# First modulation of the last two pairs of k tiles: sums over partitions on VectorE with a 32x32 transpose, their first row on ScalarE

## The chip, the cores and the metric

The kernel runs on one core of one Trainium2 chip. The metric is the device time of one execution in microseconds (us). Five engines work side by side, each through a queue of its own that it takes in order: TensorE (PE, with its weight loads as PEld), VectorE (DVE), ScalarE (ACT), GpSimd (POOL) and SyncE (SP), which here issues nearly all transfers. An engine that comes to an instruction whose input is not there yet waits, and everything behind that instruction in its queue waits with it. A difference of 0.2% (1.9 us) is about what a measurement of this kernel can tell from no change.

## What is computed

One block of a decoder on 512 tokens of 1024 features, in float32. What matters here is its first step: a normalised input is scaled and shifted by vectors that come from a conditioning vector `c`, and the result `h` is projected.

```python
cs = jax.nn.silu(c)                                   # (1, 1024)
mod = cs @ ada_w[l] + ada_b[l]                        # (1, 6 * 1024)
sh_m, sc_m, gt_m, sh_f, sc_f, gt_f = jnp.split(mod, N_MOD, axis=-1)
h = modulate(rmsnorm(x, norm_mix_g[l]), sh_m, sc_m)   # h * (1 + scale) + shift
proj = h @ w_in[l]
...
h = modulate(rmsnorm(x, norm_ffn_g[l]), sh_f, sc_f)
```

`sh_m` and `sc_m` are needed before any projection can start; `sh_f` and `sc_f` only for the second half of the block. Everything after `proj` (retention, a short convolution, the merge, a feed-forward part) is untouched by the change.

## The kernel before

**Products in three parts.** Every float32 matrix is split into a rounded high part and the rest (names ending in `_h` and `_l`; for the activations `Hh` and `Hl`), and a product is made of three matmuls, low by high, high by low, high by high. TensorE works on these from the first microseconds to the last.

**The start, by pairs of k tiles.** The 1024 features of `h` are 8 k tiles of 128. Up to line 551 the kernel works on the first projections (two column tiles each of `c`, `u`, `b` and one of `k`, seven accumulators in all) by k tile, as the data come in: pair 0 (k tiles 0 and 1), then pairs 2, 4 and 6. In this part all five queues are in the order in which the program is written (`strict = True`, line 352, up to line 552): nothing is moved by a scheduler.

For a pair `j`, the columns of `ada_w` for its shifts and scales are 4 x 128 numbers wide, and each partition holds 8 of the 1024 rows. So the vector-matrix product is done in two steps:

- `ada_sum` (line 185): VectorE multiplies the first row by its factor in `cs` (`tensor_scalar_mul`, into a tile `acc_m`) and adds the other seven, one `scalar_tensor_tensor` each, 128x512. `some_sums` (line 478) spreads this over the loop: rows 0 and 1, then (behind the low part of k tile `j-2`) rows 2 and 3, then rows 4 to 7.
- `mod_sums` (line 396): TensorE sums over the partitions. `acc_m` is the stationary side, in four blocks of 128 columns, against a 128x128 tile of ones; the four results lie in the PSUM tile `mods`, by feature. In the trace each of these float32 matmuls has two records, so a pair has eight.

`mod_cols` (line 225) then makes the scale and shift of both k tiles from `mods` with three small VectorE instructions (`a_m`, `s_m`, `a_m`), ScalarE applies them (`h_hi` writes `Hh`, `h_full` the full `h` over the input tile `xT`), and VectorE takes the difference (`h_lo`, `Hl`).

The loop over `j` in (2, 4, 6) is short and its order is the order on every queue:

```python
        steps = products(j - 1)
        run(steps, 14)
        ...
        mod_sums(sums[j], both, j > 2)
        w_lo("c", j)
        mod_cols("m", j, mods.rearrange("p (i n) -> p i n", n=P)[:, :, 0])
        for k in (j, j + 1):
            h_hi(k)
            h_full(k)
        ...
        run(steps)
        some_sums(j + 2, 0, 2)
        h_lo(j)
        run(products(j))
```

`products(k)` are the 21 matmuls of k tile `k`, three parts of seven. In an even k tile the part with `Hl` comes last; in an odd one too, and the sums of the next pair over partitions stand on TensorE's queue just ahead of those last seven (`run(steps, 14)`).

**A second way to sum over partitions** exists further down for the second modulation and the gates: `quarters` (line 244) makes two small constant tiles (`quart_sum` 128x128 and `quart_own` 128x4), `quarter_sums` (line 254) sums 32 columns at a time behind a 32x32 transpose in one VectorE instruction (128x16 from 128x512), and one matmul with `quart_sum` and two small VectorE instructions finish it (`mod_whole`, line 265). `quarters` is called at line 837, in the later part.

Of the kernel before, what the change touches and what calls it, by code (L numbers as in the profile page):

```python
# [11 lines left out]
F32 = mybir.dt.float32  # L12
# [4 lines left out]
ALU = mybir.AluOpType  # L17
AX = mybir.AxisListType

P = 128  # L20
# [50 lines left out]
def block_kernel(ctx, tc, x, c, positions, ada_w, ada_b, norm_mix_g, w_in, conv_w, ret_w_out,  # L71
# [3 lines left out]
    pe, vec, act, pool, sync = (InTurn(tc, e) for e in (nc.tensor, nc.vector, nc.scalar, nc.gpsimd,  # L75
                                                        nc.sync))
    mm, transpose = pe.matmul, pe.transpose
# [5 lines left out]
    sp = ctx.enter_context(tc.tile_pool(name="sp", bufs=4))  # L83
# [15 lines left out]
    def aux(name, shape=None):  # L99
        return ps.tile(shape or [P, S], F32, tag="aux", bufs=2, name=name)  # L100
# [64 lines left out]
    cs = cp.tile([P, KT], F32, name="cs")  # L165
# [19 lines left out]
    def ada_sum(pieces, n, name, a=None, k0=0):  # L185

        first = a is None
        if first:
            a = sp.tile([P, n], F32, tag="adaacc", bufs=2, name=f"acc_{name}")
        for k, w in enumerate(pieces, k0):  # L190
            if first and k == k0:
                vec.tensor_scalar_mul(a, w, cs[:, k:k + 1])
            else:
                vec.scalar_tensor_tensor(a, w, cs[:, k:k + 1], a, ALU.mult, ALU.add)
        return a
# [7 lines left out]
    def ada_load(f, j):  # L203


        s0 = 0 if f == "m" else 3
        cols = slice(j * P, (j + 2) * P)
        ada_raw[f, j] = pieces = []
        for k in range(0, KT, 4):
            raw = wp.tile([P, 4, 2, 2 * P], F32, tag="raw", bufs=3, name=f"ada_{f}{j}_{k}")  # L210
            for q, i in ((q, i) for q in range(0, 4, 2) for i in range(2)):
                load_raw.last = sync.dma_start(raw[:, q:q + 2, i],
                                               aw6[:, k + q:k + q + 2, s0 + i, cols])
            pieces += [raw[:, q].rearrange("p s n -> p (s n)") for q in range(4)]

    def mod_scale(f, k, col):
        g = (R_GM if f == "m" else R_GF) + k
        vec.scalar_tensor_tensor(mod["a_" + f][:, k:k + 1], col, vecs[0][:, g:g + 1],
                                 mod["b_" + f][:, k:k + 1], ALU.mult, ALU.add)

    def mod_shift(f, k, cols, n):
        r = R_ADA + ADA["sh_" + f] // P + k
        vec.tensor_tensor(mod["s_" + f][:, k:k + n], cols, vecs[0][:, r:r + n], ALU.add)

    def mod_cols(f, j, pt):

        mod_scale(f, j, pt[:, 2:3])
        mod_shift(f, j, pt[:, 0:2], 2)
        mod_scale(f, j + 1, pt[:, 3:4])

    def mod_gains(f):

        r0 = R_ADA + ADA["sc_" + f] // P
        g0 = R_GM if f == "m" else R_GF
        vec.scalar_tensor_tensor(mod["b_" + f], vecs[0][:, r0:r0 + KT], 1.0, vecs[0][:, g0:g0 + KT],
                                 ALU.add, ALU.mult)
# [4 lines left out]
    QP = P // 4  # L241
    quart, own, mod_q = {}, {}, {}

    def quarters():
        quart["sum"] = cp.tile([P, 4, QP], F32, name="quart_sum")
        cols = sp.tile([P, QP], F32, tag="quart", bufs=1, name="quart_cols")
        vec.tensor_reduce(cols, ident.rearrange("p (q c) -> p c q", q=4), axis=AX.X, op=ALU.add)
        vec.tensor_copy(quart["sum"], cols.unsqueeze(1).to_broadcast([P, 4, QP]))
        quart["own"] = cp.tile([P, 4], F32, name="quart_own")
        vec.tensor_reduce(quart["own"], ident.rearrange("p (q c) -> p q c", q=4), axis=AX.X,  # L250
                          op=ALU.add)
        quart["f"] = cp.tile([P, 2 * D // QP], F32, name="quart_f")

    def quarter_sums(o, a):

        vec.tensor_reduce(o, a.rearrange("p (j c) -> p j c", c=QP), axis=AX.X, op=ALU.add,
                          apply_transpose=True)
# [86 lines left out]
    def w_load(k):  # L344
        for n in "cubk":
            cols = P if n == "k" else 2 * P
            w_raw[n, k] = scr(f"w_{n}0_{k}", F32, [P, 2, cols])
            load_raw.last = sync.dma_start(
                w_raw[n, k], wi[k * P:(k + 2) * P, COL[n]:COL[n] + cols].rearrange(
                    "(k p) n -> p k n", p=P))  # L350
# [31 lines left out]
    def x_by_feature(t, h, copy):  # L382
        for q in range(2):
            copy(xT[2 * h + q][:, :, t * P:(t + 1) * P], txs[t, h][:, 2 * q:2 * q + 2])

    kp, mods = aux("p_k00"), aux("mods")

    def mod_row(j, k, banks, first, cols=range(4)):


        for i in cols:
            mm(banks[i % 2][:, i * P:(i + 1) * P], lhsT=ada_raw["m", j][k][:, i * P:(i + 1) * P],
               rhs=cs[:, k:k + 1].to_broadcast([P, P]),
               start=first and (i == 0 or i == 1 and banks is apart), stop=False)

    def mod_sums(a, banks, first, cols=range(4)):

        for i in cols:
            mm(banks[i % 2][:, i * P:(i + 1) * P], lhsT=a[:, i * P:(i + 1) * P], rhs=ones32,
               start=first and i == 0, stop=i == 3 or i == 2 and banks is apart)  # L400

    apart, both = (mods, kp), (mods, mods)
# [23 lines left out]
    x_by_feature(2, 0, act.copy)  # L426
    x_by_feature(2, 1, act.copy)
    mod_gains("m")
    mod_row(0, 1, apart, False)
    a = ada_sum(ada_raw["m", 0][2:6], 4 * P, "m0", None, 2)  # L430
    x_by_feature(3, 0, act.copy)
# [18 lines left out]
    def w_hi(n, k):  # L450
        raws[n, k] = w_raw.pop((n, k))
        wt[n, k] = [slot(f"w_{n}0_{k}_{z}", F32R, raws[n, k].shape) for z in "hl"]
        act.copy(wt[n, k][0], raws[n, k])

    def w_lo(n, k):
        hi, lo = wt[n, k]
        vec.tensor_tensor(lo, raws.pop((n, k)), hi.bitcast(F32), ALU.subtract)
# [3 lines left out]
    def h_hi(k):  # L461

        h32[k] = xT[k // 2][:, k % 2]
        hist.append(act.activation(Hh[:, k, :], h32[k], AF.Identity,
                                   scale=mod["a_m"][:, k:k + 1], bias=mod["s_m"][:, k:k + 1]))
# [6 lines left out]
    def h_lo(k):  # L472
        hlast.append(vec.tensor_tensor(Hl[:, k, :], h32.pop(k), Hh[:, k, :].bitcast(F32),
                                       ALU.subtract))

    sums = {}

    def some_sums(j, k0, k1):

        if j < KT:  # L480
            sums[j] = ada_sum(ada_raw["m", j][k0:k1], 4 * P, f"m{j}", sums.get(j), k0)

    def products(k):
        ops = []
        parts = (0, 1, 2) if k % 2 else (1, 0, 2)
        for part in parts:
            x = (Hl if part == 2 else Hh)[:, k, :]
            for n, i in grp:
                w = wt[n, k - k % 2][1 if part == 0 else 0][:, k % 2, :]
                at = k == 0 and part == parts[0], k == KT - 1 and part == 2  # L490
                ops.append((gps[n, i], w[:, i * P:(i + 1) * P], x, at, (n, i)))
        if k == KT - 1:
            ops.sort(key=lambda o: grp.index(o[4]))
        if k == 0:
            order = {"c": 0, "u": 1, "b": 2, "k": 3}
            ops = sorted(ops[:14], key=lambda o: order[o[4][0]]) + ops[14:]
        for o, w, x, (first, last), _ in ops:
            yield mm(o, lhsT=w, rhs=x, start=first, stop=last)

    def run(steps, n=21):  # L500
        for _, _ in zip(range(n), steps):
            pass
# [27 lines left out]
    for j in range(2, KT, 2):  # L530
        if j + 2 < KT:
            ada_load("m", j + 2)
            w_load(j + 2)
        steps = products(j - 1)
        run(steps, 14)
        if j == 2:
            mod_row(j, 7, both, True)
        else:
            some_sums(j, 4, KT)
        for n in "cubk":  # L540
            w_hi(n, j)
        mod_sums(sums[j], both, j > 2)
        w_lo("c", j)
        mod_cols("m", j, mods.rearrange("p (i n) -> p i n", n=P)[:, :, 0])
        for k in (j, j + 1):
            h_hi(k)
            h_full(k)
        for n in "ubk":
            w_lo(n, j)
# [4 lines that stand above are left out]
        some_sums(j + 2, 2, 4)  # L554
        h_lo(j + 1)
# [278 lines left out]
    m_a = [None] * KT  # L834
    with tc.issue_after(hlast[-1].ins):
        mod_gains("f")
        quarters()
    merged = [None] * KT
    for p in range(KT // 2):
        sg = {}  # L840
# [46 lines left out]
    for p in range(KT // 2):  # L887
# [4 lines left out]
        for i, pt in proj(conv_w_out[0], 2 * p * P, conv_in, None, f"yb{p}"):  # L892
            f = 2 * p + i
# [300 lines left out]
    for h in range(2):  # L1194
# [15 lines left out]
        for t, cs in tm_gemm(ffn_w_down[0], af, f0, nf, h, groups, nf - 6, "dn", True):  # L1210
# [11 lines left out]
            i = 1 + cs.start // HS  # L1222
# [44 lines left out]
```

## Time and profile before

| | |
|---|---|
| time, median of 3 runs | 942.69 us (942.5 to 943.29) |
| time of the profiled execution | 942.61 us |
| its span in the profile | 940.8 us, so 1.81 us lie around the span |
| TensorE (PE) busy | 931.3 us, 99% of the span |
| TensorE weight loads (PEld) | 778.0 us, 83% |
| VectorE (DVE) busy | 634.2 us, 67% |
| ScalarE (ACT) busy | 359.9 us, 38% |
| granted TensorE clock, mean | 0.998 of full speed |
| VectorE busy from 20 to 40 us, from 40 to 60 us | 17.51 and 17.05 of 20 us |
| VectorE busy from 70 to 100 us | 29.8 of 30 us |

The profile is one execution. A line of the timeline gives the start of an instruction (or a group of like ones, xN), how long it took, its engine, the line of the kernel (L62 and L64 are the helper that records every operation), the operation, output<-input by tile names, and in square brackets how long the engine sat idle before it and what ended that. Matmuls overlap: a 128x512 matmul lasts 0.39 us in the records, and the next starts 0.23 us later, so the distance from start to start is the one to count. The same holds for VectorE and ScalarE, where the next independent instruction starts some 0.1 us before the end that is shown.

### The profile page before, as it was taken

The page shows a single profiled execution, that of the slowest core. Times are in us where ns is not written, and L with a number is a line of the kernel's source. Part 1 is how long each engine was busy: PE and PEld are TensorE (multiplying, and loading weights), DVE is VectorE, ACT ScalarE, POOL GpSimd, SP SyncE. Part 2 cuts the span into 40 slices and gives each one's busy share as a digit, 9 for nine tenths or more (in the row PEclk, how much of TensorE's full clock was granted, in tenths as well). Part 3 has the DMA queues.
Part 4 walks back from the last instruction along what each step waited for, and adds up shares of the span by engine and source line. Part 5 has one row for each costly group of instructions (what it writes and reads, how often), then busy time and mean ns, then how long its engine had stood idle before and what let it go on. Part 6 is the DMA issues. An engine that isn't in the chain of part 4 may idle for free.

```text
span 940.8 us, 11007 instructions
## 1 busy us (share of the span) xinstructions
PE 931.3 (99%) x4325; PEld 778.0 (83%) x4325; DVE 634.2 (67%) x977; ACT 359.9 (38%) x529; POOL 13.8 (1%) x34
## 2 busy tenths in 40 slices
PE   8999999999999999999999999999999999999997
PEld 8888888888888888888888888988888888888886
DVE  5889784898768756554674457668687546883346
ACT  7535432554444423222233236423443234433224
POOL 2000000000000000000000000000000000000000
PEclk9999999999999999999999999999999999999999
DMA  9943413321642346766463540446556652553202
GB/s 325 338 150 112 148 53 101 101 77 69 208 160 90 134 134 223 225 201 202 142 216 113 180 151 28 140 150 199 199 186 225 225 175 90 179 179 111 68 23 90
DMA packets 113491, 144.04 MB, mean 153 GB/s; under 512 B 4308, under 2 KB 93440, under 8 KB 112416
## 3 DMA queue, kind: packets, MB, share of 16 engines
q1 hardware_dynamic: 111472, 133.45, 43.3%
q0 software_dynamic: 1824, 9.63, 2.8%
q8 instruction: 34, 0.56, 0.2%
q10 hardware_dynamic: 144, 0.26, 0.1%
q14 instruction: 17, 0.14, 0.0%
HBM read 132.83 MB, written 10.49 MB: 152 GB/s over the span
## 4 chain that ended last, share of the span: by engine, by line
PE 97%; DMA 1%; DVE 1%; ACT 1%; issue 0%; SPq 0%; ACTq 0%
PE p_fu L64 13%; PE p_fg L64 12%; PE p_g L64 5%; PE p_yb L64 5%; PE p_v L64 5%; PE p_gb L64 5%; PE p_ya L64 5%; PE dn_t L64 5%; PE p_ga L64 5%; PE p_q L64 5%; PE p_k L64 4%; PE p_u L64 3%; PE p_b L64 3%; PE p_c L64 3%; PE dn_b L64 3%; PE dn L64 3%
## 5 line engine op out<-in xcount | busy, mean ns | idle before, releaser
L64 PE MATMUL p_fu<-Gh,w_fu_l 128*128 128x512 f32 x160 | 62.4, 390 | 0.0
L64 PE MATMUL p_fu<-Gl,w_fu_h 128*128 128x512 f32 x160 | 62.3, 389 | 0.0
L64 PE MATMUL p_fu<-Gh,w_fu_h 128*128 128x512 f32 x160 | 62.3, 389 | 0.0
L64 PE MATMUL p_fg<-Gh,w_fg_l 128*128 128x512 f32 x160 | 62.2, 389 | 0.0
L64 PE MATMUL p_fg<-Gh,w_fg_h 128*128 128x512 f32 x160 | 62.2, 389 | 0.0
L64 PE MATMUL p_fg<-Gl,w_fg_h 128*128 128x512 f32 x160 | 62.2, 389 | 0.0
L64 DVE TENSOR_TENSOR w_fg_l<-w_fg,w_fg_h 128x1024 fp32r<-128x1024 f32 x20 | 24.3, 1218 | 35.0 <-ACT w_fg_h L64 35.0
L64 ACT CAST w_fu_h<-w_fu 128x1024 fp32r<-128x1024 f32 x20 | 21.1, 1054 | 62.1 <-PE p_fu L64 39.6
L64 ACT ACTIVATE fg<-p_fg 128x512 f32<-128x512 f32 x22 | 13.1, 598 | 71.5 <-PE p_fg L64 71.5
L64 DVE TENSOR_TENSOR fg<-p_fu,fg 128x512 f32<-128x512 f32 x22 | 15.2, 690 | 35.5 <-PE p_fu L64 35.5
L64 DVE TENSOR_TENSOR w_b_l<-w_b,w_b_h 128x1024 fp32r<-128x1024 f32 x18 | 22.0, 1221 | 23.1 <-ACT w_b_h L64 23.1
L64 PEld LDWEIGHTS p_fu<-Gh,w_fu_l 128*128 128x128 f32 x160 | 30.0, 188 | 6.3
L64 PEld LDWEIGHTS p_fg<-Gh,w_fg_l 128*128 128x128 f32 x160 | 30.0, 188 | 6.3
L64 PEld LDWEIGHTS p_fg<-Gl,w_fg_h 128*128 128x128 f32 x160 | 30.0, 188 | 6.2
L64 PEld LDWEIGHTS p_fu<-Gh,w_fu_h 128*128 128x128 f32 x160 | 30.0, 188 | 6.2
L64 PEld LDWEIGHTS p_fg<-Gh,w_fg_h 128*128 128x128 f32 x160 | 30.0, 188 | 6.2
L64 PEld LDWEIGHTS p_fu<-Gl,w_fu_h 128*128 128x128 f32 x160 | 30.0, 188 | 6.2
L64 DVE TENSOR_TENSOR w_bl<-w_bl 128x512 f32<-128x512 f32 x32 | 22.0, 687 | 12.6 <-DMA w_bl<-in_ffn_w_down_dram 12.3
L64 DVE SCALAR_TENSOR_TENSOR acc_f<-ada_f,cs,acc_f 128x512 f32<-128x512 f32 x28 | 21.0, 750 | 8.8 <-DMA ada_f<-in_ada_w_dram 7.9
L64 ACT CAST sh<-sm 128x512 fp32r<-128x512 f32 (+3 forms) x32 | 14.7, 459 | 31.5 <-DVE sm L64 31.4
L64 DVE TENSOR_TENSOR w_fu_l<-w_fu,w_fu_h 128x1024 fp32r<-128x1024 f32 x20 | 24.4, 1220 | 3.4 <-ACT w_fu_h L64 3.4
L64 ACT CAST w_b_h<-w_b 128x1024 fp32r<-128x1024 f32 x18 | 18.9, 1049 | 19.1 <-issue 7.9
(429 smaller groups left out, 2716.5 us busy)
## 6 DMA issues: line engine op xcount, KB each, us to landing
w_fg<-in_ffn_w_gate_dram SPq DMA_DIRECT2D x11, 1024.0 KB, 5.3
w_fu<-in_ffn_w_up_dram SPq DMA_DIRECT2D x11, 1024.0 KB, 5.2
ada_m<-in_ada_w_dram SPq DMA_DIRECT2D x32, 256.0 KB, 5.3
w_bl<-in_ffn_w_down_dram SPq DMA_DIRECT2D x16, 512.0 KB, 4.7
blocks<-w_bl POOLq DMA_DIRECT2D x8, 1024.0 KB, 4.6
ada_f<-in_ada_w_dram SPq DMA_DIRECT2D x32, 256.0 KB, 4.6
w_t<-blocks SPq DMA_DIRECT2D x8, 1024.0 KB, 5.7
w_b<-in_ffn_w_down_dram SPq DMA_DIRECT2D x6, 1024.0 KB, 5.0
```

The lines of the kernel that those rows point to most:

```text
L64: self.last = op(*args, **kw)
```

## The change

It has three parts.

- The first row of `ada_sum` for pairs 4 and 6 is multiplied on ScalarE (`act.mul`) in place of VectorE (`tensor_scalar_mul`). The other rows stay.
- For pairs 4 and 6 the sum over partitions goes the second way: `quarter_sums` on VectorE, one matmul with `quart_sum` that has 16 columns, and two small VectorE instructions ahead of `mod_cols`. The four matmuls with ones go. Pair 2 stays as it was.
- `quarters` is called at the start, behind `mod_gains("m")`, no longer ahead of the second half.

```diff
@@ ada_sum
-            if first and k == k0:
+            if first and k == k0 and name in ("m4", "m6"):
+                act.mul(a, w, cs[:, k:k + 1])
+            elif first and k == k0:
                 vec.tensor_scalar_mul(a, w, cs[:, k:k + 1])
@@ the start
     mod_gains("m")
+    quarters()
     mod_row(0, 1, apart, False)
@@ new functions
+    def mod_quarters(j):
+        n = 4 * P // QP
+        part = sp.tile([P, n], F32, tag="mpart", bufs=1, name=f"mpart{j}")
+        quarter_sums(part, sums[j])
+        mm(mods[:, 0:n], lhsT=quart["sum"].rearrange("p q c -> p (q c)"), rhs=part, start=True,
+           stop=True)
+
+    def mod_own(j):
+        each = sp.tile([P, 4, 4], F32, tag="meach", bufs=1, name=f"meach{j}")
+        vec.tensor_tensor(each, mods[:, 0:16].rearrange("p (n q) -> p n q", q=4),
+                          quart["own"].unsqueeze(1).to_broadcast([P, 4, 4]), ALU.mult)
+        cols = sp.tile([P, 4], F32, tag="mown", bufs=1, name=f"mown{j}")
+        vec.tensor_reduce(cols, each, axis=AX.X, op=ALU.add)
+        mod_cols("m", j, cols)
@@ the loop over pairs
-        mod_sums(sums[j], both, j > 2)
-        w_lo("c", j)
-        mod_cols("m", j, mods.rearrange("p (i n) -> p i n", n=P)[:, :, 0])
+        if j == 2:
+            mod_sums(sums[j], both, False)
+            w_lo("c", j)
+            mod_cols("m", j, mods.rearrange("p (i n) -> p i n", n=P)[:, :, 0])
+        else:
+            mod_quarters(j)
+            w_lo("c", j)
+            mod_own(j)
@@ ahead of the second half
         mod_gains("f")
-        quarters()
```

Where this lands on the queues is seen at three places. The number behind a tile's name is that of its buffer. First ScalarE's queue in the round of pair 2, from the second k tile's `Hh` on (`xT_123` is the input of k tiles 2 and 3). Before:

```order
L62 ACTIVATE Hh<-xT_123,s_m,a_m 128x512
L62 ACTIVATE xT_123<-xT_123,s_m,a_m 128x512
L62 CAST w_c_4_h<-w_c_4_381 128x512
L62 CAST w_u_4_h<-w_u_4_383 128x512
L62 CAST w_b_4_h<-w_b_4_385 128x512
L62 CAST w_k_4_h<-w_k_4_387 128x256
```

The same place now:

```order
L62 ACTIVATE Hh<-xT_123,s_m,a_m 128x512
L62 ACTIVATE xT_123<-xT_123,s_m,a_m 128x512
L62 ACTIVATE acc_m_448<-ada_m_0_378,cs 128x512
L62 CAST w_c_4_h<-w_c_4_388 128x512
L62 CAST w_u_4_h<-w_u_4_390 128x512
L62 CAST w_b_4_h<-w_b_4_392 128x512
L62 CAST w_k_4_h<-w_k_4_394 128x256
```

The first row of pair 4 (`acc_m_448`) stands behind all four ACTIVATEs that apply the modulation of pair 2, and ahead of the high parts of pair 4's weights.

Second VectorE's queue at the same time, from the last weight of pair 2 to the shift of pair 4. Before:

```order
L62 TENSOR_TENSOR w_k_2_l<-w_k_2_335,w_k_2_h 128x256
L62 TENSOR_SCALAR acc_m_441<-ada_m_0_371,cs 128x512
L62 SCALAR_TENSOR_TENSOR acc_m_441<-ada_m_0_371,cs,acc_m_441 128x512
L62 TENSOR_TENSOR Hl<-xT_123,Hh 128x512
L62 SCALAR_TENSOR_TENSOR acc_m_441<-ada_m_0_371,cs,acc_m_441 128x512 x2
L62 TENSOR_TENSOR Hl<-xT_123,Hh 128x512
L62 SCALAR_TENSOR_TENSOR acc_m_441<-ada_m_4_376,cs,acc_m_441 128x512 x4
L62 TENSOR_TENSOR w_c_4_l<-w_c_4_381,w_c_4_h 128x512
L62 SCALAR_TENSOR_TENSOR a_m<-mods,vecs,b_m 128x1
L62 TENSOR_TENSOR s_m<-mods,vecs 128x2
```

The same place now:

```order
L62 TENSOR_TENSOR w_k_2_l<-w_k_2_342,w_k_2_h 128x256
L62 SCALAR_TENSOR_TENSOR acc_m_448<-ada_m_0_378,cs,acc_m_448 128x512
L62 TENSOR_TENSOR Hl<-xT_123,Hh 128x512
L62 SCALAR_TENSOR_TENSOR acc_m_448<-ada_m_0_378,cs,acc_m_448 128x512 x2
L62 TENSOR_TENSOR Hl<-xT_123,Hh 128x512
L62 SCALAR_TENSOR_TENSOR acc_m_448<-ada_m_4_383,cs,acc_m_448 128x512 x4
L62 TENSOR_REDUCE mpart_524<-acc_m_448 128x16
L62 TENSOR_TENSOR w_c_4_l<-w_c_4_388,w_c_4_h 128x512
L62 TENSOR_TENSOR meach_528<-mods,quart_own 128x16
L62 TENSOR_REDUCE mown_530<-meach_528 128x4
L62 SCALAR_TENSOR_TENSOR a_m<-mown_530,vecs,b_m 128x1
L62 TENSOR_TENSOR s_m<-mown_530,vecs 128x2
```

The first row is gone, and the second row, which reads what ScalarE writes, keeps its place ahead of `Hl`; three new instructions stand between the sums and the scale. The round of pair 4 looks the same with 4 and 6 in place of 2 and 4.

Third the start of VectorE's queue, where pair 0's sums begin. Before:

```order
L62 TENSOR_SCALAR x_136<-x_136,r_127 128x1024
L62 SCALAR_TENSOR_TENSOR b_m<-vecs 128x8
L62 TENSOR_SCALAR acc_m_264<-ada_m_0_138,cs 128x512
L62 SCALAR_TENSOR_TENSOR acc_m_264<-ada_m_0_138,cs,acc_m_264 128x512
L62 SCALAR_TENSOR_TENSOR acc_m_264<-ada_m_4_143,cs,acc_m_264 128x512 x2
```

The same place now:

```order
L62 TENSOR_SCALAR x_136<-x_136,r_127 128x1024
L62 SCALAR_TENSOR_TENSOR b_m<-vecs 128x8
L62 TENSOR_REDUCE quart_cols<-ident 128x32
L62 COPY quart_sum<-quart_cols 128x128
L62 TENSOR_REDUCE quart_own<-ident 128x4
L62 TENSOR_SCALAR acc_m_271<-ada_m_0_138,cs 128x512
L62 SCALAR_TENSOR_TENSOR acc_m_271<-ada_m_0_138,cs,acc_m_271 128x512
```

Three instructions of `quarters` now stand ahead of pair 0's first row.

## Rows read from the trace of the kernel before

**Rows 1.** The page: busy time of TensorE (us, share of the span, instructions), and the shares of the chain of work that ended last, by engine.

```profile
PE 931.3 (99%) x4325; PEld 778.0 (83%) x4325; DVE 634.2 (67%) x977; ACT 359.9 (38%) x529; POOL 13.8 (1%) x34
...
PE 97%; DMA 1%; DVE 1%; ACT 1%; issue 0%; SPq 0%; ACTq 0%
```

**Rows 2.** All waits of TensorE over the whole span: engine and what it was about to do <- who ended the wait: us in total, times, longest.

```profile
PE idle L64 <- POOL ident masks.py:199: 1.5, 1, 1.5
PE tx L62 <- DVE x L62: 0.9, 1, 0.9
PE p_c L62 <- ACT Hh L62: 0.4, 1, 0.4
PE y L64 <- ACT sh L64: 0.2, 1, 0.2
```

**Rows 3.** Timeline of TensorE in the rounds of pairs 2 and 4 (start us, us, engine, line, operation, output<-input, count).

```profile
33.79 0.62 PE L62 MATMUL p_c<-Hl,w_c_h 128*128 128x512 f32 x2
...
38.55 1.05 PE L62 MATMUL mods<-ones,acc_m 128*128 128x128 f32 x8
39.36 0.71 PE L62 MATMUL p_c<-Hl,w_c_h 128*128 128x512 f32 x2
39.91 0.63 PE L62 MATMUL p_u<-Hl,w_u_h 128*128 128x512 f32 x2
40.37 0.62 PE L62 MATMUL p_b<-Hl,w_b_h 128*128 128x512 f32 x2
...
44.24 0.62 PE L62 MATMUL p_c<-Hl,w_c_h 128*128 128x512 f32 x2
...
49.00 1.05 PE L62 MATMUL mods<-ones,acc_m 128*128 128x128 f32 x8
```

**Rows 4.** Timeline of VectorE in the same rounds.

```profile
31.05 0.48 DVE L62 TENSOR_SCALAR acc_m<-ada_m,cs 128x512 f32<-128x512 f32 x1
31.57 0.75 DVE L62 SCALAR_TENSOR_TENSOR acc_m<-ada_m,cs,acc_m 128x512 f32<-128x512 f32 x1
32.24 0.69 DVE L62 TENSOR_TENSOR Hl<-xT,Hh 128x512 fp32r<-128x512 f32 x1
...
34.89 3.11 DVE L62 SCALAR_TENSOR_TENSOR acc_m<-ada_m,cs,acc_m 128x512 f32<-128x512 f32 x4
37.91 0.68 DVE L62 TENSOR_TENSOR w_c_l<-w_c,w_c_h 128x512 fp32r<-128x512 f32 x1
...
39.78 0.15 DVE L62 TENSOR_TENSOR s_m<-mods,vecs 128x2 f32<-128x2 f32 x1
...
42.02 0.75 DVE L62 SCALAR_TENSOR_TENSOR acc_m<-ada_m,cs,acc_m 128x512 f32<-128x512 f32 x1
42.69 0.69 DVE L62 TENSOR_TENSOR Hl<-xT,Hh 128x512 fp32r<-128x512 f32 x1
...
45.35 3.11 DVE L62 SCALAR_TENSOR_TENSOR acc_m<-ada_m,cs,acc_m 128x512 f32<-128x512 f32 x4
```

**Rows 5.** Timeline of ScalarE in the same rounds.

```profile
31.91 0.82 ACT L62 ACTIVATE xT<-xT,s_m,a_m 128x512 f32<-128x512 f32 x1
...
39.96 0.82 ACT L62 ACTIVATE Hh<-xT,s_m,a_m 128x512 fp32r<-128x512 f32 x1 [4.23 <-DVE s_m L62]
...
42.37 0.81 ACT L62 ACTIVATE xT<-xT,s_m,a_m 128x512 f32<-128x512 f32 x1
43.09 0.61 ACT L62 CAST w_c_h<-w_c 128x512 fp32r<-128x512 f32 x1
```

**Rows 6.** Single tiles elsewhere in the span, with the kinds of instruction that the change adds: engine, operation, output<-input, count: duration in ns least/median/most, first and last start in us; shapes.

```profile
L64 ACT ACTIVATE o<-x,nf_r x4: 722/724/726, 926.3 to 936.4; 128x512 f32<-128x512 f32 x4
...
L64 DVE TRANSPOSE_TENSOR_REDUCE quart_f<-acc_f x4: 700/711/711, 362.8 to 429.9; 128x16 f32<-128x512 f32 x4
...
L64 DVE TENSOR_TENSOR mod_each<-mod_f,quart_own x1: 209/209/209, 450.7 to 450.7; 128x64 f32<-128x64 f32 x1
L64 DVE TENSOR_REDUCE mod_cols<-mod_each x1: 206/206/206, 451.2 to 451.2; 128x16 f32<-128x64 f32 x1
```

**Rows 7.** Timeline of TensorE where the second modulation's matmul with `quart_sum` (64 columns) stands between two projections.

```profile
449.16 0.33 PE L64 MATMUL mod_f<-quart_f,quart_sum 128*128 128x64 f32 x2
...
449.61 0.40 PE L64 MATMUL p_gb<-Hl,w_gb_h 128*128 128x512 f32 x1
449.85 0.40 PE L64 MATMUL p_gb<-Hh,w_gb_h 128*128 128x512 f32 x1
```

**Rows 8.** Timeline of VectorE at the start and at 61 us, where `quarters` stands before, and of TensorE's sums for pair 0.

```profile
12.85 0.16 DVE L62 SCALAR_TENSOR_TENSOR b_m<-vecs 128x8 f32<-128x8 f32 x1
13.27 0.49 DVE L62 TENSOR_SCALAR acc_m<-ada_m,cs 128x512 f32<-128x512 f32 x1 [0.26 <-DMA ada_m<-in_ada_w_dram]
...
14.70 2.46 DVE L62 SCALAR_TENSOR_TENSOR acc_m<-ada_m,cs,acc_m 128x512 f32<-128x512 f32 x4 [0.16 <-DMA ada_m<-in_ada_w_dram]
...
17.19 0.61 PE L62 MATMUL mods<-ones,acc_m 128*128 128x128 f32 x4
...
61.56 0.37 DVE L64 TENSOR_REDUCE quart_cols<-ident 128x32 f32<-128x128 f32 x1
...
62.05 0.22 DVE L64 COPY quart_sum<-quart_cols 128x128 f32<-128x128 f32 x1
...
62.52 0.28 DVE L64 TENSOR_REDUCE quart_own<-ident 128x4 f32<-128x128 f32 x1
```


## The prediction, made before the changed kernel ran

> **What bounds the kernel now.** I read the page first: TensorE is busy for 99% of the span and makes up 97% of the chain that ended last [rows 1]. Then all its waits: four in the whole execution, 3.0 us together, the last of the first three before 20 us [rows 2]. So from there on a matmul less is time won, a wait added is time lost, and work of another engine costs nothing as long as it comes before TensorE asks for it. Last the timelines of the three engines from 31 to 50 us, for how much earlier each input comes than it is asked for. That cover is small: VectorE ends `Hl` of k tile 2 at 32.24 + 0.69 = 32.93 and TensorE starts on it at 33.79, 0.86 later; the four last rows of pair 4's sum end at 34.89 + 3.11 = 38.00 and TensorE sums them at 38.55, 0.55 later [rows 3, 4].
>
> **Matmuls removed.** From the first of the eight records of pair 4's sum (38.55) to the second pair of matmuls behind them (39.91) are 1.36 us; two such matmuls alone take 40.37 - 39.91 = 0.46, so the block costs 0.90 [rows 3]. The one matmul in its place is nearest to that of the second modulation, which has 64 columns and not 16: from it to the second matmul behind it are 449.61 - 449.16 = 0.45, of which the matmul between takes 449.85 - 449.61 = 0.24, so it costs 0.21 [rows 7]. Saved 0.69 a pair; at most 0.90 if it cost nothing.
>
> The Trainium skill ("TensorE: Matmul & The Clock Gate", section "Back-to-back issue gap") gives 134 cycles at 2.4 GHz for 128 columns and about 60 for up to 64; worked out from that, eight records are 0.45 us, two are 0.05, and a pair would save 0.40. The rows have 0.90 and 0.21, and the measurement decides; by the page the sum below would be 0.6 us higher.
>
> **First row on ScalarE: a wait ahead of `Hl`.** In `acc_m` the second row is added to the first, so VectorE's second instruction of the pair now waits for ScalarE. ScalarE's queue holds the product behind the four ACTIVATEs that modulate pair 2. The last of them starts at 31.91, and what follows it starts 43.09 - 42.37 = 0.72 later in the next round, so the product starts at 32.63 [rows 5]. The same form (128x512, a factor by partition) takes 0.72 at the end of the kernel [rows 6]; bounds are the cast's 0.61 and the ACTIVATE's 0.82 [rows 5]. It ends at 33.35; with 0.03 from the end of `s_m` (39.78 + 0.15) to ScalarE's start at 39.96 [rows 4, 5] as the step from engine to engine, VectorE goes on at 33.38. Before, that instruction started at 31.57 [rows 4]: VectorE is 1.81 late, although it has one product less. Queued behind the wait are `Hl` of both k tiles and the rest of the sum.
> - `Hl` of k tile 2 ends at 32.93 + 1.81 = 34.74. With 0.05 to TensorE that is 34.79 against 33.79: TensorE waits 1.00.
> - TensorE is then at the sum at 39.55, its former 38.55 plus 1.00. VectorE ends the sum at 38.00 + 1.81 = 39.81.
>
> The Trainium skill ("ScalarE: Activation LUTs", section "Rules for kernel authors") says to put multiplications on VectorE and not on ScalarE, since VectorE is faster by the element. The durations agree, 0.72 against 0.48 [rows 4, 6]; read by that rule alone the move would cost the difference, and that is the first rival below.
>
> **The transposed sum and the two small instructions.** The transposed reduce of the same size takes 0.71 [rows 6] and starts 0.03 behind the sum: it ends at 40.55, so TensorE's one matmul starts at 40.60 in place of 39.55, a second wait of 1.05. Then the shift and scale:
> - TensorE, after 0.21 for that matmul and seven at 0.23, asks for `Hh` of k tile 4 at 40.60 + 0.21 + 1.61 = 42.42.
> - The matmul's result is there at 40.60 + 0.33 [rows 7], but VectorE first does `w_c_l` (0.68, starting 0.1 before the reduce's end), so it is free at about 41.07. The multiplication with `quart_own` and the reduce take 0.21 each for 64 columns [rows 6]; 16 can only be less. With 0.03 between dependent ones, the first ends at 41.28, the second at 41.52, `a_m` starts at 41.55, `s_m` ends at 41.84, and `Hh` runs on ScalarE from 41.87 for 0.82 [rows 5], to 42.69. TensorE starts at 42.74: a third wait of 0.32.
>
> Round of pair 4: 1.00 + 1.05 + 0.32 - 0.69 = **+1.68**.
>
> **Round of pair 6.** ScalarE is 41.87 - 39.96 = 1.91 late, so the product runs from 43.09 + 1.91 = 45.00 to 45.72, and VectorE goes on at 45.75 where it was at 42.02 [rows 4, 5]: 3.73 late. `Hl` of k tile 4 ends at 42.69 + 0.69 + 3.73 = 47.11; TensorE, 1.68 late, asks at 44.24 + 1.68 = 45.92 and waits 1.24 to 47.16. It is at the sum at 49.00 + 2.92 = 51.92 [rows 3]; the transposed sum ends at 45.35 + 3.11 + 3.73 + 0.03 + 0.71 = 52.93: with 0.05 a wait of 1.06. The third wait is again 0.32. 1.24 + 1.06 + 0.32 - 0.69 = **+1.93**.
>
> **`quarters` at the start.** Its three instructions take 0.37, 0.22 and 0.28 at 61 us [rows 8]. Behind `b_m` they run from 12.93 to about 13.75, so pair 0's first row starts near 13.67, not 13.27, and the group that waited for a transfer until 14.70 starts at 14.98. The sum ends 0.28 later than 17.16; TensorE took it at once (17.19) [rows 8], though its first matmuls there need only the first half of the columns, which is summed sooner. I take **+0.2**; bounds 0 (the waits for transfers hide it) and 0.8 (all of it). Taken away at 61 us, where VectorE is full, it gives nothing, since TensorE doesn't wait there [rows 2].
>
> **What costs nothing.** The high parts of the next weights stand 0.72 later on ScalarE; `w_c_h` of pair 6 started at 43.09 without a wait [rows 5] and is used only with its own `Hh`, after the sum at 49.00 [rows 3]. No transfer is moved; those that wait for `ada_w` tiles to be freed follow VectorE's delay and stay ahead of users that are as late. Behind 61 us nothing is nearer to TensorE than before: VectorE is 0.3 us late against it and has 0.9 less to do.
>
> **Sum:** 1.68 + 1.93 + 0.2 = +3.8 on the profiled execution's 942.61 us (span 940.8 and 1.81 around it; the median is 0.08 higher): **946.4 us**, 0.4% slower.
>
> **Rivals.**
> 1. *The product costs only its own length.* ScalarE would have to reach it when VectorE did, at 31.05; then VectorE is late by 0.72 - 0.48 + 0.03 = 0.27. `Hl` still has cover (0.86). The transposed sum ends at 38.00 + 0.27 + 0.74 = 39.01 against 38.55: waits 0.5 and 0.3 a round against 0.69 saved, +0.1 each, with the start 943.0 us. This is the case that ends on the other side; it decides by ScalarE's queue: up to a delay of 0.8 us for VectorE `Hl` waits for nothing. Against it stand the four ACTIVATEs ahead of the product in queue order, for it nothing but that their inputs might be ready sooner, which `s_m` at 39.78 excludes [rows 4, 5].
> 2. *The edit does what it is written for:* the first row off VectorE makes room (0.52 us) for the transposed sum, no wait is added, and the matmuls saved are time won: 2 x 0.69 - 0.2 = 1.2 us, 941.4 us. It needs the product to be done before about 31.3, when ScalarE still has two ACTIVATEs ahead. Even so it stays within 0.2%; faster by more takes the full 1.8 us and a free start.
> 3. *Waits cost more than their length.* If the matmuls behind each wait start anew as the first ones behind the old sum did (39.91 - 39.36 = 0.55 for two in place of 0.46) [rows 3], six waits add 0.5 us, with the start at its upper bound 0.6 more: 947.5 us.
>
> **How the numbers follow.** Forecast 0.73, rival 1 0.07, rival 2 0.05, rival 3 0.13, and 0.02 for a gain by a way I don't see. The range holds the forecast and rival 3. Below: product at the cast's 0.61 (-0.2), start free (-0.2), both third waits gone because 16 columns take less than 64 (-0.6), matmul for nothing (-0.4): 945.0. Above 947.5. Slower by over 0.2% (beyond 944.6): 0.86; within: 0.12; faster: 0.02. 0.2% is about what a measurement of this kernel can tell from no change.
>
> **What would show it.** In the changed profile: waits of TensorE for `Hl` of about 1.0 and 1.2 us (for `p_c`, ended by VectorE), two for `mods` of about 1.05, two small ones for `Hh`; VectorE idle some 2.3 us ahead of the second row, ended by ScalarE's `acc_m`, in both rounds; pair 0's sum on TensorE 0.2 us later than 17.19. It is wrong if VectorE doesn't stand still there, or if `Hl` comes in time although it does.

## The result

| | time, median | span of the profiled execution |
|---|---|---|
| before | 942.69 us (5 runs, 942.5 to 943.29) | 940.8 us |
| changed | 946.84 us (5 runs, 946.65 to 947.05) | 944.7 us |

The changed kernel is slower: the ratio of the times is 1.0045, with a 95% interval of 1.0035 to 1.0056. The profiled execution took 946.84 us against 942.61; 3.9 us of the 4.2 lie inside the span, and the other 0.3 around it (2.14 us there against 1.81). Those 0.3 us come with the product on ScalarE: in all 53 runs of the seven kernels that have it, 2.12 to 2.31 us lie around the span, and in all 53 runs of the two that don't (before and vector_row, below) 1.79 to 1.96. Among the seven is row_only, which changes nothing else. What these 0.3 us are, no trace shows.

**Where TensorE waits now.** The view of all its waits over the whole span, as in [rows 2]:

```profile
PE p_c L62 <- DVE Hl L62: 1.8, 2, 0.9
PE mods L62 <- DVE mpart L62: 1.5, 2, 0.8
PE idle L64 <- POOL ident masks.py:199: 1.5, 1, 1.5
PE tx L62 <- DVE x L62: 1.0, 1, 1.0
PE p_c L62 <- ACT Hh L62: 0.4, 1, 0.4
PE y L64 <- ACT sh L64: 0.2, 1, 0.2
```

Two lines are new, two waits each: for `Hl`, and for the transposed sum `mpart`. The four old ones are as they were; the two small waits for `Hh` that the prediction looked for as well are too short for this view. All four new waits lie in the stretch that the prediction counts as the rounds of pairs 4 and 6. The timeline of TensorE there, with the start of pair 0's sum ([rows 8] has it at 17.19 before) and the first matmul behind the loop, against [rows 3]:

```profile
17.30 0.82 PE L62 MATMUL mods<-ones,acc_m 128*128 128x128 f32 x4
...
19.41 0.73 PE L62 MATMUL p_c<-Hh,w_c_h 128*128 128x512 f32 x2 [0.40 <-ACT Hh L62]
...
33.87 0.39 PE L62 MATMUL p_k<-Hh,w_k_l 128*128 128x512 f32 x1
35.09 0.73 PE L62 MATMUL p_c<-Hl,w_c_h 128*128 128x512 f32 x2 [0.83 <-DVE Hl L62]
35.66 0.62 PE L62 MATMUL p_u<-Hl,w_u_h 128*128 128x512 f32 x2
...
39.76 0.39 PE L62 MATMUL p_k<-Hh,w_k_h 128*128 128x512 f32 x1
40.91 0.40 PE L62 MATMUL mods<-mpart,quart_sum 128*128 128x16 f32 x2 [0.76 <-DVE mpart L62]
41.16 0.72 PE L62 MATMUL p_c<-Hl,w_c_h 128*128 128x512 f32 x2
...
42.64 0.40 PE L62 MATMUL p_k<-Hl,w_k_h 128*128 128x512 f32 x1
42.95 0.73 PE L62 MATMUL p_c<-Hh,w_c_h 128*128 128x512 f32 x2
...
47.36 0.73 PE L62 MATMUL p_c<-Hl,w_c_h 128*128 128x512 f32 x2 [0.93 <-DVE Hl L62]
...
53.18 0.40 PE L62 MATMUL mods<-mpart,quart_sum 128*128 128x16 f32 x2 [0.74 <-DVE mpart L62]
...
64.88 0.39 PE L64 MATMUL p_v<-w_v_h,Hl 128*128 128x512 f32 x1
```

The bracket shows less than a wait costs, because the record of the matmul ahead runs into the wait. From start to start: behind the matmul at 33.87 the next was due 0.23 later, at 34.10, and came at 35.09, 0.99 late. The sum was due at 39.99 and came at 40.91, 0.92 late. `Hh` of k tile 4 was used at 42.95, 23.54 us after the first projection (19.41); before it was 41.06 - 19.09 = 21.97, by two rows of the kernel before's timeline that are not among [rows 3] (the third is its first matmul behind the loop):

```profile
19.09 0.73 PE L62 MATMUL p_c<-Hh,w_c_h 128*128 128x512 f32 x2 [0.40 <-ACT Hh L62]
...
41.06 0.61 PE L62 MATMUL p_c<-Hh,w_c_h 128*128 128x512 f32 x2
...
61.03 0.39 PE L64 MATMUL p_v<-w_v_h,Hl 128*128 128x512 f32 x1
```

So the round of pair 4 cost 1.57 us. What holds TensorE up is seen on VectorE, against [rows 4]:

```profile
13.00 0.16 DVE L62 SCALAR_TENSOR_TENSOR b_m<-vecs 128x8 f32<-128x8 f32 x1
13.08 0.37 DVE L62 TENSOR_REDUCE quart_cols<-ident 128x32 f32<-128x128 f32 x1
13.48 0.23 DVE L62 COPY quart_sum<-quart_cols 128x128 f32<-128x128 f32 x1
13.63 0.28 DVE L62 TENSOR_REDUCE quart_own<-ident 128x4 f32<-128x128 f32 x1
13.82 0.48 DVE L62 TENSOR_SCALAR acc_m<-ada_m,cs 128x512 f32<-128x512 f32 x1
...
33.68 0.75 DVE L62 SCALAR_TENSOR_TENSOR acc_m<-ada_m,cs,acc_m 128x512 f32<-128x512 f32 x1 [2.06 <-ACT acc_m L62]
34.35 0.68 DVE L62 TENSOR_TENSOR Hl<-xT,Hh 128x512 fp32r<-128x512 f32 x1
...
37.00 3.11 DVE L62 SCALAR_TENSOR_TENSOR acc_m<-ada_m,cs,acc_m 128x512 f32<-128x512 f32 x4
40.15 0.71 DVE L62 TRANSPOSE_TENSOR_REDUCE mpart<-acc_m 128x16 f32<-128x512 f32 x1
40.78 0.65 DVE L62 TENSOR_TENSOR w_c_l<-w_c,w_c_h 128x512 fp32r<-128x512 f32 x1
41.35 0.17 DVE L62 TENSOR_TENSOR meach<-mods,quart_own 128x16 f32<-128x16 f32 x1
41.55 0.17 DVE L62 TENSOR_REDUCE mown<-meach 128x4 f32<-128x16 f32 x1
...
41.90 0.15 DVE L62 TENSOR_TENSOR s_m<-mown,vecs 128x2 f32<-128x2 f32 x1
...
45.95 0.75 DVE L62 SCALAR_TENSOR_TENSOR acc_m<-ada_m,cs,acc_m 128x512 f32<-128x512 f32 x1 [2.23 <-ACT acc_m L62]
...
52.41 0.71 DVE L62 TRANSPOSE_TENSOR_REDUCE mpart<-acc_m 128x16 f32<-128x512 f32 x1
```

VectorE stands still for 2.06 and 2.23 us, released by ScalarE's `acc_m`; `Hl` follows at 34.35, the transposed reduce at 40.15. And on ScalarE, against [rows 5], the product runs where its place in the queue puts it, right behind the last ACTIVATE of the modulation:

```profile
32.22 0.81 ACT L62 ACTIVATE xT<-xT,s_m,a_m 128x512 f32<-128x512 f32 x1
32.94 0.71 ACT L62 ACTIVATE acc_m<-ada_m,cs 128x512 f32<-128x512 f32 x1
...
42.09 0.82 ACT L62 ACTIVATE Hh<-xT,s_m,a_m 128x512 fp32r<-128x512 f32 x1 [6.35 <-DVE s_m L62]
...
44.49 0.82 ACT L62 ACTIVATE xT<-xT,s_m,a_m 128x512 f32<-128x512 f32 x1
45.21 0.71 ACT L62 ACTIVATE acc_m<-ada_m,cs 128x512 f32<-128x512 f32 x1
```

### The profile page after: what moved, and what is told of

Same layout as the page of the kernel before. It is cut to its first block, busy times and chain, and to the rows that moved or that the text cites. A ratio compares the mean times of both kernels' runs of the same rounds, so it can differ in the third digit from the quotient of the medians.

```text
span 944.7 us, 10987 instructions
## 1 busy us (share of the span) xinstructions
PE 931.8 (99%) x4313; PEld 776.4 (82%) x4313; DVE 636.3 (67%) x981; ACT 360.7 (38%) x531; POOL 13.8 (1%) x34
## 4 chain that ended last, share of the span: by engine, by line
PE 94%; DVE 2%; DMA 2%; ACT 1%; issue 1%; SPq 0%; DVEq 0%; ACTq 0%
PE p_fu L64 13%; PE p_fg L64 12%; PE p_g L64 5%; PE p_yb L64 5%; PE p_v L64 5%; PE p_gb L64 5%; PE p_ya L64 5%; PE dn_t L64 5%; PE p_ga L64 5%; PE p_q L64 5%; PE p_k L64 4%; PE p_b L64 3%; PE p_u L64 3%; PE p_c L64 3%; PE dn_b L64 3%; PE dn L64 3%
## 5 line engine op out<-in xcount | busy, mean ns | idle before, releaser
L64 DVE TENSOR_TENSOR sm<-st,dec 128x512 f32<-128x512 f32 (+3 forms) x32 | 15.6, 487 | 16.6 <-PE st L64 16.2
```

The lines of the kernel that those rows point to most:

```text
L64: self.last = op(*args, **kw)
```

## The experiments

The theory: VectorE's second row waits for a product that ScalarE's queue holds back, `Hl` and the sum are queued behind that wait, and the longer sum then comes late as well. The rivals are a price of the parts themselves: the product on the slower engine, the transposed reduce on the path, the constants at the start. In the table the first two columns are starts read from TensorE's timeline of each profiled execution: the first projection (`p_c`) and the first matmul behind the loop over the pairs (`p_v`). The third is their difference, so it holds all rounds and nothing of the start. Each ratio is to runs of the kernel before on the same chip (medians 942.59 to 942.69 us).

| kernel | first p_c | first p_v | between | time, median | ratio to before, 95% |
|---|---|---|---|---|---|
| before | 19.09 | 61.03 | 41.94 | 942.69 | |
| changed | 19.41 | 64.88 | 45.47 | 946.84 | 1.0035 to 1.0056 |
| vector_row | 19.47 | 61.57 | 42.10 | 942.86 | 0.9995 to 1.0012 |
| row_only | 19.07 | 63.85 | 44.78 | 945.68 | 1.0022 to 1.0047 |
| row_between | 19.25 | 60.35 | 41.10 | 942.02 | 0.9986 to 1.0004 |
| hl_first | 19.12 | 63.62 | 44.50 | 945.54 | 1.0021 to 1.0046 |
| quarters_first | 19.00 | 64.47 | 45.47 | 946.42 | 1.0028 to 1.0054 |
| row_between_ones | 18.77 | 60.68 | 41.91 | 943.03 | 0.9994 to 1.0012 |
| row_between_quarters_first | 18.91 | 60.04 | 41.13 | 942.14 | 0.9988 to 1.0006 |

From `p_v` to the end of the span all nine take 879.65 to 879.82 us: nothing is given back or lost later.

**vector_row: the product back on VectorE, the rest of the change kept.**

```diff
-            if first and k == k0 and name in ("m4", "m6"):
-                act.mul(a, w, cs[:, k:k + 1])
-            elif first and k == k0:
+            if first and k == k0:
                 vec.tensor_scalar_mul(a, w, cs[:, k:k + 1])
```

> The changed kernel with the first row of pairs 4 and 6 back on VectorE; the transposed sums and the early quarters stay. If the cost is VectorE standing still for ScalarE's product (my theory), the waits for Hl vanish, the transposed sum ends about 0.3 us after TensorE asks for it, and what the removed matmuls save pays for that: 0.2 us won in all on the two rounds, 0.3 lost at the start, 942.8 us. If the transposed sum on the path were the cause (rival), only the waits for Hl would be given back, about 2.2 us of the 946.8: 944.6 us.

The median is 942.86 us. The waits for `Hl` are gone, and those for the sum are short (waits of TensorE, then VectorE's timeline):

```profile
PE mods L62 <- DVE mpart L62: 0.4, 2, 0.3
```

```profile
35.46 3.11 DVE L62 SCALAR_TENSOR_TENSOR acc_m<-ada_m,cs,acc_m 128x512 f32<-128x512 f32 x4
38.60 0.71 DVE L62 TRANSPOSE_TENSOR_REDUCE mpart<-acc_m 128x16 f32<-128x512 f32 x1
```

So the transposed sum isn't the cause by itself: with VectorE on time it comes 0.35 to 0.41 us late, and with the slow starts behind such a wait (below) that is about what the removed matmuls save. The rounds take 42.10 us, 0.16 above before, where 0.2 below was expected; the time stays even. The second and third parts of the change, without the first, are thus no gain.

**row_only: the kernel before with nothing but the product on ScalarE.**

```diff
-            if first and k == k0:
+            if first and k == k0 and name in ("m4", "m6"):
+                act.mul(a, w, cs[:, k:k + 1])
+            elif first and k == k0:
                 vec.tensor_scalar_mul(a, w, cs[:, k:k + 1])
```

> The kernel before with one edit: the first row of pairs 4 and 6 on ScalarE. Theory: VectorE is 1.8 us late in pair 2's round, TensorE waits 1.0 us for Hl and 0.2 for the sum, then 1.0 and 0.2 in the next round, with 0.1 more behind each wait for Hl: +2.6 us, 945.3 us. If the product cost only its own length on the path (0.72 instead of 0.48 us, rival), both rounds together cost 0.5 us at most: 942.7 to 943.2 us.

945.68 us, and 2.84 us more in the rounds than before (2.6 expected). VectorE goes on at 33.35, 2.24 us after it became free, and TensorE gets `Hl` at 34.76; the prediction had 33.38 and 34.79 (VectorE, then TensorE):

```profile
33.35 0.75 DVE L62 SCALAR_TENSOR_TENSOR acc_m<-ada_m,cs,acc_m 128x512 f32<-128x512 f32 x1 [2.24 <-ACT acc_m L62]
```

```profile
34.76 0.74 PE L62 MATMUL p_c<-Hl,w_c_h 128*128 128x512 f32 x2 [0.83 <-DVE Hl L62]
...
39.84 1.16 PE L62 MATMUL mods<-ones,acc_m 128*128 128x128 f32 x8
```

A product that costs only its own length is excluded. The parts don't add up: 2.84 (product) and 0.16 (transposed sum) make 3.00, and both together cost 45.47 - 41.94 = 3.53. The sum has 0.55 us of cover before [rows 3, 4], and the late product uses it up: here the old sum is already 0.14 and 0.18 late from start to start. So the reduce's 0.71 then counts in full.

**row_between: the product one ACTIVATE into the modulation, not four.**

```diff
+    def first_row(j):
+        if j < KT:
+            sums[j] = sp.tile([P, 4 * P], F32, tag="adaacc", bufs=2, name=f"acc_m{j}")
+            act.mul(sums[j], ada_raw["m", j][0], cs[:, 0:1])
...
         for k in (j, j + 1):
             h_hi(k)
+            if k == j:
+                first_row(j + 2)
             h_full(k)
...
-        some_sums(j + 2, 0, 2)
+        some_sums(j + 2, 1, 2)
         h_lo(j)
```

(Not shown: `ada_sum` goes back to its form before, since `first_row` now issues the product. The same holds for hl_first.)

> The changed kernel with ScalarE's product moved between the first Hh and the rest of the modulation (one ACTIVATE ahead of it in place of four). Theory: the product ends before VectorE asks for it, VectorE gains 0.5 us of room, the transposed sum is ready when TensorE comes to it, and each round ends 0.5 us earlier than before; with 0.3 us lost at the start 942.0 us. If the product on ScalarE or the transposed sum were dear by themselves (rivals), nothing much changes: 945 us or more. Open is whether the first row's data have landed so early; if not, ScalarE stands still with Hh of the second k tile behind it.

942.02 us, as expected. That is clearly faster than the changed kernel; against the kernel before, the interval (0.9986 to 1.0004) holds no change. ScalarE runs the product from 30.39, VectorE needs it at 31.40 and stands still no longer, and TensorE comes to the sum without a wait (ScalarE, VectorE, TensorE):

```profile
29.67 0.82 ACT L62 ACTIVATE Hh<-xT,s_m,a_m 128x512 fp32r<-128x512 f32 x1 [2.04 <-DVE s_m L62]
30.39 0.71 ACT L62 ACTIVATE acc_m<-ada_m,cs 128x512 f32<-128x512 f32 x1
31.00 0.80 ACT L62 ACTIVATE xT<-xT,s_m,a_m 128x512 f32<-128x512 f32 x1
```

```profile
31.40 0.74 DVE L62 SCALAR_TENSOR_TENSOR acc_m<-ada_m,cs,acc_m 128x512 f32<-128x512 f32 x1
32.06 0.68 DVE L62 TENSOR_TENSOR Hl<-xT,Hh 128x512 fp32r<-128x512 f32 x1
...
37.85 0.71 DVE L62 TRANSPOSE_TENSOR_REDUCE mpart<-acc_m 128x16 f32<-128x512 f32 x1
```

```profile
38.72 0.29 PE L62 MATMUL mods<-mpart,quart_sum 128*128 128x16 f32 x2
...
40.33 0.39 PE L62 MATMUL p_k<-Hl,w_k_h 128*128 128x512 f32 x1
40.66 0.73 PE L62 MATMUL p_c<-Hh,w_c_h 128*128 128x512 f32 x2
```

With the same instructions on the same engines, 45.47 us between the two marks became 41.10, 0.84 less than before: in the rounds the whole loss is the product's place in ScalarE's queue. The first row's data had landed in time.

**hl_first: `Hl` taken out of the wait.** The product stays where the change has it; VectorE's second row moves behind the first `Hl`.

```diff
-        some_sums(j + 2, 0, 2)
+        first_row(j + 2)
         h_lo(j)
         run(products(j))
-        some_sums(j + 2, 2, 4)
+        some_sums(j + 2, 1, 4)
         h_lo(j + 1)
```

(`first_row` as above, called here and not in the modulation.)

> The changed kernel with VectorE's second row moved behind the first Hl, so that Hl no longer stands behind the wait for ScalarE; product and transposed sum stay where they are. Theory: VectorE still stands still until ScalarE's product, so the wait for Hl goes and the wait for the sum grows to about 1.3 us; only VectorE's 0.6 us of Hl per round now lies inside its idle time: 1.2 us won in all, 945.6 us. If the order of Hl behind the wait were the whole cost (rival), both waits for Hl and what follows them go: 944.6 us.

945.54 us. The waits for `Hl` are gone, and the time is not: the sum comes 1.58 and 1.67 us late instead, from start to start, where 1.3 was expected (waits of TensorE, then VectorE's timeline).

```profile
PE mods L62 <- DVE mpart L62: 2.9, 2, 1.5
```

```profile
31.26 0.69 DVE L62 TENSOR_TENSOR Hl<-xT,Hh 128x512 fp32r<-128x512 f32 x1
33.40 2.33 DVE L62 SCALAR_TENSOR_TENSOR acc_m<-ada_m,cs,acc_m 128x512 f32<-128x512 f32 x3 [1.45 <-ACT acc_m L62]
```

VectorE still stands still for 1.45 us, 0.6 less, since one `Hl` now fills part of it. The wait moved to the next thing that TensorE asks for. So not the order behind the wait but the time at which the product ends sets the loss.

**quarters_first: the constants in VectorE's idle time ahead of the first reciprocal.**

```diff
     mod_gains("m")
-    quarters()
...
     busy(18)
+    quarters()
```

> The changed kernel with the two constant tiles made in VectorE's idle time ahead of the first reciprocal, not behind mod_gains. Theory: pair 0's sum is no longer late, 0.3 us won, and the two rounds are as slow as before: 946.5 us. If the constants' place cost nothing (rival: the start is set by transfers), 946.8 us as the changed kernel; if they were the main cost, 943 us.

946.42 us; the rounds are 45.47 us, exactly as in the changed kernel, and the first projection starts at 19.00. Over all nine kernels the four with the constants behind `mod_gains` start it at 19.12 to 19.47 (mean 19.31), the five others at 18.77 to 19.09 (mean 18.97). Single starts scatter by as much as these means differ, and the times don't tell it: the intervals of quarters_first and the changed kernel overlap. Counted from the start of `b_m`, which stands just ahead of the constants' place, the scatter of what comes before is left out: then it is 6.40 to 6.43 us to the first projection in three of the four (6.72 in hl_first, where `b_m` started earliest, at 12.40), and 6.16 to 6.24 in the five others. So about 0.2 us at the start are the constants.

**row_between_ones: the product in its better place, with the old sums.** The edit of row_between made in the kernel before.

> The kernel before, its sums with ones, with only the first row of pairs 4 and 6 on ScalarE, behind the first Hh. Theory: VectorE gains 0.5 us a round, but TensorE waits for nothing there, so the time stays: 942.6 us. If a product on ScalarE were dear by itself (rival), this would be slower as well, toward the 945.7 us of the run with the product behind all four ACTIVATEs; if room on VectorE were worth something by itself, 941.6 us.

943.03 us, no difference from before that can be told, and 41.91 us in the rounds against 41.94. VectorE has 0.5 us more room, which nobody asks for. In the rounds the product on ScalarE costs nothing in that place, and gains nothing; the 0.3 us around the span are there in this kernel too (2.12 to 2.21 us in its 11 runs).

**row_between_quarters_first: both mends.** The edits of row_between and quarters_first together.

> Both mends at once: the product behind the first Hh, and the constants in VectorE's idle time at the start. Theory: the 0.3 us of the start come on top of the 0.5 us a round, 941.6 us, 0.1% faster than before; if the start is set by transfers, 942.0 us.

942.14 us. The profiled execution shows both gains (first projection at 18.91, rounds of 41.13 us, 939.7 us, the shortest span of the nine profiled executions), but the median is not under row_between's 942.02, and its interval, 0.9988 to 1.0006, holds no change. That this version beats the kernel before is not shown; if it does, by less than 0.2%.

## Why the prediction was right

The forecast was 946.4 us in a range of 945.0 to 947.5; measured 946.84. Its steps one by one, on TensorE from start to start:

| step | foretold, pair 4 | measured | foretold, pair 6 | measured |
|---|---|---|---|---|
| wait for `Hl` | 1.00 | 0.99 | 1.24 | 1.09 |
| wait for the sum | 1.05 | 0.92 | 1.06 | 0.90 |
| wait for `Hh` | 0.32 | 0.08 | 0.32 | 0.08 |
| slow starts behind the waits | none in the sum | 0.25 | none in the sum | 0.54 |
| matmuls saved | -0.69 | -0.67 | -0.69 | -0.67 |
| round | 1.68 | 1.57 | 1.93 | 1.96 |

Both rounds together were foretold at 3.61 us and measured at 3.53, the start at 0.2 and 0.32, of which 0.17 are left when counted from `b_m`. The round of pair 6 is measured up to `p_v`, and the slow start behind pair 4's wait for `Hh` counts in it.

- **The product's place** was read from the order of ScalarE's queue and the rows of its ACTIVATEs. It took 0.71 us, and VectorE went on at 33.68; with the start 0.3 us later than before that is the foretold 33.38. VectorE stood still for 2.06 and 2.23 us, where the prediction looked for some 2.3. The step of 0.05 us from VectorE to TensorE, for which it named no row, was 0.06 for `Hl` (35.03 to 35.09) and 0.05 for the sum (40.86 to 40.91).
- **Matmuls saved.** In row_between, where the new matmul follows without a wait, it costs 0.25 us: its start to that of the last of the seven behind it is 40.33 - 38.72 = 1.61, and from the last matmul ahead (38.49) 1.84, against 1.59 for seven alone. Before it was 0.92 in the same measure, so 0.67 is saved.

  The Trainium skill ("TensorE: Matmul & The Clock Gate", section "Back-to-back issue gap") would have given 0.40 by its cycles, which it states for an isolated matmul, taken once for each record. By the rows it is 0.67, as [rows 3] and [rows 7] had said.
- **The third wait was too long by a quarter microsecond.** The step that failed was the way from the sum's matmul to `Hh`: 2.14 us foretold (40.60 to 42.74), 2.04 measured in both rounds (40.91 to 42.95 in the first). Most of that is the two small instructions, taken at 0.21 us each, the rows' value for 64 columns; with 16 columns they took 0.17. The other 0.14 us are TensorE's own: it asked for `Hh` later, 1.96 us after the start of that matmul and not 1.82, since the seven behind it started slowly and the matmul took 0.25 and not 0.21.
- **Rival 3 held as a mechanism, but hardly adds to the time.** The matmuls behind a wait do start anew: 35.66 - 35.09 = 0.57 us for two, against 0.46 in a run. Over the seven behind a wait it is 0.13 or 0.14 for `Hl` and `Hh` (1.72 or 1.73 us against 1.59), and 0.12 for the sum (40.91 to 42.64 against 38.72 to 40.33 without a wait in row_between: 1.73 against 1.61). That is 0.79 for the six waits, where the rival had 0.5 and the sum nothing. But the six waits together were 0.93 shorter than foretold, and mostly for this reason: a wait ends when VectorE or ScalarE is ready, so a TensorE that starts slowly asks later and waits less. What sets the time is the path over VectorE and ScalarE, and there the working held: with the start's 0.32, the foretold 40.60 for the sum's matmul is 40.92, and it came at 40.91. Twice 0.10 us less on the way to `Hh` and one slow start behind the last wait, which no later wait takes up, make 3.61 - 0.20 + 0.14 = 3.55, against 3.53. That these two errors nearly cancel is luck; that the other slow starts don't show is not.
- **Rival 1** (the product costs its own length) needed ScalarE to be free when VectorE is. row_only excluded it: the product cost 2.84 us there, where its own length would have cost 0.5 at most.

  The Trainium skill ("ScalarE: Activation LUTs", section "Rules for kernel authors") advises against multiplications on ScalarE because of the speed by the element, which it gives for bf16. The durations of this case, in float32, agree with it, 0.71 us against 0.48, but by row_between_ones they cost nothing in the rounds; the place in the queue cost 2.84 us.
- **Rival 2** (the edit does what it is written for) comes near once the product stands early: row_between has 0.84 us less in the rounds, of the 1.38 (2 x 0.69) that it gave there. Its condition, no wait added, isn't met even then. In row_between's rows above, `Hh` of k tile 4 was due 0.23 us behind the matmul at 40.33, at 40.56, and came 0.10 late, with a slow start behind it; the next round has the same. vector_row shows that the transposed sum needs the room that the product leaves on VectorE: without it it is late by about as much as it saves.

0.3 of the 0.44 us between forecast and measurement lie outside the span. The prediction carried the kernel before's 1.81 us over unchanged; with a product on ScalarE it is 2.1 to 2.3 in every run, and the profile doesn't show what is there.

## What to carry to other kernels

Work that moves to an idle engine is not done when that engine is idle, but where it stands in its queue: look what is ahead of it there and when that is released, and compare that with the time at which the old engine needed it. A mean share of busy time (ScalarE's 38%) says nothing on this. Of two parts of a change, test each alone and both together, because the first can use up the cover that made the second free, as here (2.84 + 0.16 against 3.53 us).

## What the runs showed that was not expected

Rival 3 had the slow starts behind a wait. Not expected was that most of them don't show in the time: where another wait follows that ends when another engine is ready, it becomes shorter by as much. Why TensorE starts slowly stays open. The clock isn't the reason: the granted clock is 1.00 in the stretch from 34.0 to 36.5 us, in the changed kernel with its wait as in the one before without.

A wait that the bracket of the timeline gives as 0.83 and 0.76 us was 0.99 and 0.92 us from start to start, so sums of brackets run low by some 0.16 us each.

And the time around the span isn't the same for every kernel: two products moved to ScalarE add 0.3 us there, in row_only and in row_between_ones alike.
